# Hybrid encoder trunk on one core: where the score rows live, which engine makes w_out's low parts, and when the pair sums are queued

## The chip, the core and the metric

The kernel runs on one core of a Trainium2 chip. The metric is the device time of one execution in microseconds (us), from runs on the chip; each run gives one time, and the table below gives the median. Beside them stands one profiled execution, whose trace all rows in this document come from.

## What is computed

Two batches, a prompt of 512 tokens and a sample of 1024, go through the same layer of 1024 channels, all in fp32. Cut to what matters:

```
h = rmsnorm(x);  z = h @ w_in                      # q 8 heads x 64, k, v 2 heads x 64, conv 2 x 512
sc = q @ k.T / 8 + bias, |q-k| <= 128              # window: 3 blocks of 128 keys
m = max(max(sc), sink)
p = exp(sc - m);  denom = sum(p) + exp(sink - m)   # one sink logit per head
a = (p / denom) @ v
c = silu(layernorm(dwconv31(ca * sigmoid(cb))))
x = x + concat(a, c) @ w_out
h = rmsnorm(x);  u = dwconv3(h @ w_up)             # 2 x 2816 columns
x = x + (silu(u[:2816]) * u[2816:]) @ w_down
y = rmsnorm(x)
```

## The kernel before

**Products.** Every fp32 operand of a large product is split into a high part (a copy rounded by ScalarE, ACT) and a low part (the difference, made by VectorE, DVE, or GpSimd, POOL). Each 128-deep step of a product is three matmuls, hi·hi, hi·lo and lo·hi. `split` (from L139) does this for a weight: the cast is L142, the subtraction L143, on DVE if `dve` is true and on POOL otherwise. `proj` (L249 to L252) issues the three matmuls for eight steps.

**Stages, with their place in the trace.** Up to about 117 us: projections of the prompt. 117 to some 376: projections of the sample as the main work, with `prompt()` beside it (attention of four blocks of 128 queries in eight units of one block and one key head, conv_norm of the convolution half, the prompt's w_out product). 300 to 680: the prompt's feed-forward up-projection (`ffn_step`) as the main work, with `sample()` beside it (attention of the sample in 16 units, the loads and splits of w_out, two conv_norms). 668 to 793: the sample's w_out product, blocks 4 to 11 of 128 rows (`out_blocks`), with conv_norm, the `pair_sums` and the first transposes beside it. 793 to 816: the turn to a wide form of the sample's up-projection, which takes sums and differences of row blocks and of weight blocks in place of one product (`scaled`, `sums_up`, `turned`, `prod` with its matmuls at L1002 to L1004). Then that up-projection and the down-projections to the end.

**What sets the order.** The main work calls `tick` after every second step of a product. `tick` adds `pace["rate"]` to an account and calls the next part of the generator at the head of `side` for each whole unit on it; the convolution taps have an account of their own. A scheduler then fixes the order in which each engine takes its instructions; on an engine it is a fixed queue, and an instruction that waits holds up all behind it. The same holds for SP's queue, which issues the DMAs. A DMA's start waits until the tile that it writes is free.

**Memory.** SBUF tiles are slots of fixed size, taken by size: 15 of 4096 bytes per partition (names q), 4 of 4224 (c), 61 of 2048 (h), 2 of 2176 (d) and 32 small ones (s). A raw weight and its two parts take a q slot each. Where h slots have run out, an h-sized tile takes a larger one. PSUM banks have the names a, u, b, c.

**Scores.** `scores` (from L496) issues two matmuls a head (L512) and one DVE instruction (L514) that adds the bias, keeps the negated sum in a row of SBUF and gives the row's minimum. In that row, column 0 holds the negated sink logit, put there once by eight DVE copies in `sink_columns` (L490), so that one exp on ACT (L523) over row and sink gives p and its sum with the sink's share. The rows are four tiles of 4096 bytes (`score_rows`, two heads each), held through the prompt's attention and again through the sample's. DVE then takes the reciprocal (L526), and ACT and POOL scale p. In `values`, TensorE turns p (L553), ACT and DVE split it (L555, L556), and TensorE multiplies it with v (L567, L568).

**conv_norm** (from L600) loads rows of the convolution, transposes them (L612), takes mean and variance on DVE, the reciprocal deviation on POOL (`rstd_of`, L126 and L127), normalizes on DVE (L618), transposes back (L624) and applies the activation on ACT (L627 to L631).

**w_out.** `split_wo` splits the sixteen 512-wide pieces of w_out. In `sample()` the argument `m % 4 < DW2` sends half of them to DVE; in `prompt()` `kc % 2 < DW` sends all to DVE, with the DW = 2 that the change leaves.

**The up-projection's evacuation.** ACT takes the middle tap of a PSUM bank (L779), DVE adds the two outer taps from the same bank (L775); then the bank is free for the next projection.

**pair_sums** (from L808), eleven of them: two loads of gated values (L811, L812), four 256-wide POOL operations (L816 to L819), four stores (L821). Their results are read in the wide stage. They wait in `side` at the rate RE = 1.4, with conv_norms put ahead of them.

**End of the out stage.** For each block the residual sum (L653), the square sum on ACT (L659), the rstd on POOL (L126, L127) and the scaling on DVE (L900); DVE also makes the weight sums (`sums_up`, L878) and the low parts of the transposes (L925 are the transposes).

Of the kernel before, what the change touches and what calls it, by code (L numbers as in the profile page):

```python
# [12 lines left out]
AF = mybir.ActivationFunctionType  # L13
ALU = mybir.AluOpType

P = 128
# [6 lines left out]
GRP = NH // NKV  # L23
# [13 lines left out]

RA, RB, RBO, RD, RN, RE = 1.2, 0.8, 2.5, 0.8, 0.95, 1.4  # L40


CA, CB = 0.9, 0.4
# [4 lines left out]
SCB, SCD = "aapa", "aaap"  # L48


WOP, WOA, DW, DW2 = 1, 5, 2, 2
NE = 2
YN = 2
OB = "uc"
# [41 lines left out]
def tile_hybrid_encoder(ctx: ExitStack, tc: tile.TileContext, xs, rel_bias, norm_attn_g, w_in,  # L96
                        attn_sink, conv_dw_w, conv_dw_b, conv_ln_g, conv_ln_b, w_out, norm_ffn_g,
                        w_up, ffn_dw_w, ffn_dw_b, w_down, norm_final_g, onehot, outs):
    nc = tc.nc
# [7 lines left out]
    sb = Slots(big, dict(q=(15, 4096), c=(4, 4224), h=(61, 2048), d=(2, 2176), s=(32, 64)))  # L107
# [3 lines left out]
    def sm(n):  # L111
        return sb.tile([n])
# [373 lines left out]
    def sink_columns():  # L486
        for h in range(0, NH, 2):
            t = sb.tile([2, NT])
            for n in range(2):
                nc.vector.tensor_copy(t[:, n, 0:1], nsink[:, h + n:h + n + 1])  # L490
            score_rows.append(t)

    def row_of(h):
        return score_rows[h // 2][:, h % 2, :]

    def scores(u):  # L496
        i, kv = divmod(u, 2)
        load_q(u)
        if blocks[min(u + 1, 2 * NB - 1) // 2][0] is blocks[i][0]:
            load_q(u + 1)  # L500
        G, b = blocks[i]
        kts = window(i)
        k0, nk = kts[0] * P, len(kts) * P
        off = (kts[0] - b + 1) * P
        q = qt.pop(u)
        negm, den = sm(GRP), sm(GRP)
        pr = []
        for j in range(GRP):
            h = kv * GRP + j
            sc = bank("attn")  # L510
            for L in range(2):
                nc.tensor.matmul(sc[:, :nk], q[:, j, :], kt[G["g"], kv][L][:, k0:k0 + nk],  # L512
                                 start=(L == 0), stop=(L == 1))
            nc.vector.tensor_tensor_reduce(  # L514
                out=row_of(h)[:, 1:1 + nk], in0=sc[:, :nk], in1=bias[h][:, off:off + nk], scale=-1.0,
                scalar=nsink[:, h:h + 1], op0=ALU.add, op1=ALU.min, accum_out=negm[:, j:j + 1])
            del sc
            if j == 1:
                yield 0.0

        for j in range(GRP):
            p = sb.tile([1 + 3 * P])
            nc.scalar.activation(p[:, :1 + nk], row_of(kv * GRP + j)[:, :1 + nk], AF.Exp, scale=-1.0,  # L523
                                 bias=negm[:, j:j + 1], accum_out=den[:, j:j + 1])
            pr.append(p)
        nc.vector.reciprocal(den[:], den[:])  # L526
# [178 lines left out]
    use.update(step="b", turn="a", attn="au", norm="au", out="u")  # L705

    def prompt():
        sink_columns()
        yield from attention(0, 8, {u: conv_norm(u - 4) for u in range(4, 8)})
        kt.clear(), vt.clear(), qt.clear(), bias.clear(), score_rows.clear()  # L710
        pace.update(rate=RBO, late=CLO)
        for n in range(2):
            for kc in range(KC):
                if (kc, n) not in wor:
                    load_wo(kc, n)
            yield 0.0
# [91 lines left out]
    def pair_sums(p):  # L808

        e, o, x, y = (sb.tile([NT]) for _ in range(4))  # L810
        nc.sync.dma_start(e[:], gt[2 * p][:])  # L811
        nc.sync.dma_start(o[:], gt[2 * p + 1][:])  # L812
        yield 0.0
        yield 0.0
        gp = nc.gpsimd.tensor_tensor
        gp(x[:, HR], e[:, HR], o[:, HR], op=ALU.add)  # L816
        gp(x[:, HL], e[:, HL], e[:, HR], op=ALU.subtract)
        gp(e[:, HR], x[:, HR], e[:, HL], op=ALU.subtract)
        gp(y[:, HL], o[:, HL], e[:, HR], op=ALU.subtract)  # L819
        for i, src in ((5, x[:, HR]), (7, x[:, HL]), (6, e[:, HR]), (3, y[:, HL])):  # L820
            nc.sync.dma_start(gb[i, p][:], src)  # L821
        yield 0.0
# [756 lines left out]
```

## Time and profile before

| | us |
|---|---|
| three runs | 1581.71, 1574.94, 1573.73 |
| their median | 1574.94 |
| the profiled execution | 1579.13 |
| its span in the trace | 1577.3 |

Its mean granted TensorE clock is 0.982. A row of the timeline reads: start in us, duration in us, engine, line, operation, the tiles out and in by name, their shapes, how many instructions in a row; and in brackets the idle time of the engine ahead of it with what ended it. A row of the table of stretches reads: from and to, length, then the busy us of PE (matmul), PEld (weight load), DVE, ACT and POOL with their instruction counts, the granted PE clock, the share of the DMA engines' time, GB/s. SPq rows are the DMA issues of SP's queue.

### The profile page before, as it was taken

The numbers are of one execution on the slowest core, as the hardware profiler recorded it, in microseconds if no ns is written. First come the engines' busy times: TensorE is split into PE (matmuls) and PEld (weight loads), VectorE is DVE, ScalarE is ACT, GpSimd is POOL, SyncE is SP. The second block draws the span as 40 slices with busy tenths as digits, with TensorE's granted clock in tenths as the row PEclk, the third lists the DMA queues.
The fourth block names the chain that finished last, engine by engine and source line by source line (L and its number), as shares of the span: only waits on it lengthen the run. The fifth ranks groups of instructions, "written<-read, shape, count | busy, mean of one in ns | idle before, by whom it ended". The sixth has DMA issues, their size and how long they took to land. (4 is left out here: it accounts for less than half of the span.)

```text
span 1577.3 us, 20139 instructions
## 1 busy us (share of the span) xinstructions
PE 1517.2 (96%) x6843; PEld 1234.2 (78%) x6843; DVE 1155.5 (73%) x1604; ACT 794.6 (50%) x1396; POOL 711.6 (45%) x558
## 2 busy tenths in 40 slices
PE   8999999799999999899979999999999999999997
PEld 6787778587888888788867888888888788888885
DVE  7998577747888895745776787778876945668883
ACT  4635545435677786624344444544445533343354
POOL 6641334324667765746533555555555000003345
PEclk9999899899999999999989999999999999999999
DMA  7573235328343435778432333333331582356644
GB/s 227 159 193 94 69 107 160 100 96 252 105 129 127 131 124 160 222 231 273 147 110 67 99 103 100 101 100 100 105 119 57 191 303 77 117 158 221 216 151 160
DMA packets 228780, 227.17 MB, mean 144 GB/s; under 512 B 13268, under 2 KB 168348, under 8 KB 228549
## 3 DMA queue, kind: packets, MB, share of 16 engines
q1 hardware_dynamic: 228677, 225.88, 45.2%
q8 instruction: 54, 0.88, 0.2%
q14 instruction: 49, 0.40, 0.1%
HBM read 164.74 MB, written 62.14 MB: 144 GB/s over the span
## 5 line engine op out<-in xcount | busy, mean ns | idle before, releaser
L143 POOL TENSOR_TENSOR q<-q,q 128x1024 fp32r<-128x1024 f32 x71 | 172.2, 2431 | 115.4 <-ACT q L142 43.0
L878 DVE TENSOR_TENSOR h<-h,h 128x512 fp32r<-128x512 f32 (+2 forms) x202 | 155.9, 805 | 64.4 <-ACT h L882 25.6
L878 POOL TENSOR_TENSOR q<-q,q 128x512 fp32r<-128x512 f32 x82 | 114.2, 1404 | 152.9 <-ACT q L988 147.7
L1334 PE MATMUL w<-h,h 128*128 128x512 f32 x462 | 181.3, 392 | 0.5 <-DVE q L1121 0.5
L1335 PE MATMUL w<-h,h 128*128 128x512 f32 x462 | 181.3, 392 | 0.0
L1336 PE MATMUL w<-h,h 128*128 128x512 f32 x462 | 181.2, 392 | 0.0
L249 PE MATMUL u<-h,q 128*128 128x512 f32 x400 | 162.4, 406 | 6.5 <-DVE h L775 4.5
L250 PE MATMUL u<-h,q 128*128 128x512 f32 x400 | 159.6, 399 | 0.0
L252 PE MATMUL u<-h,q 128*128 128x512 f32 x384 | 152.4, 397 | 1.9 <-POOL q L143 1.8
L1002 PE MATMUL w<-h,q 128*128 128x512 f32 x372 | 147.7, 397 | 3.5 <-ACT h L1083 1.6
L1004 PE MATMUL w<-h,q 128*128 128x512 f32 x372 | 147.1, 395 | 0.6 <-POOL q L878 0.6
L292 DVE SCALAR_TENSOR_TENSOR c<-c,cvw,c 128x512 f32<-128x512 f32 x184 | 137.9, 750 | 2.5
L875 POOL TENSOR_TENSOR q<-q,q 128x1024 f32<-128x1024 f32 x12 | 32.9, 2752 | 236.9 <-DVE q L875 220.2
L1003 PE MATMUL w<-h,q 128*128 128x512 f32 x350 | 137.7, 393 | 0.0
L882 ACT CAST h<-h 128x512 fp32r<-128x512 f32 x120 | 71.8, 619 | 95.4 <-DVE h L878 41.2
L249 PE MATMUL b<-h,q 128*128 128x512 f32 x256 | 103.7, 405 | 1.9 <-DVE d L322 1.6
L142 ACT CAST q<-q 128x1024 fp32r<-128x1024 f32 x72 | 75.3, 1050 | 59.5 <-DMA q<-in_w_in 23.9
L1334 PEld LDWEIGHTS w<-h,h 128*128 128x128 f32 x462 | 86.8, 188 | 20.5 <-ACT h L882 0.9
L250 PE MATMUL b<-h,q 128*128 128x512 f32 x256 | 102.1, 399 | 0.0
L1336 PEld LDWEIGHTS w<-h,h 128*128 128x128 f32 x462 | 86.7, 188 | 19.6
L1335 PEld LDWEIGHTS w<-h,h 128*128 128x128 f32 x462 | 86.8, 188 | 19.5
L252 PE MATMUL b<-h,q 128*128 128x512 f32 x240 | 95.9, 400 | 0.0
(427 smaller groups left out, 3819.5 us busy)
## 6 DMA issues: line engine op xcount, KB each, us to landing
q<-in_w_up SPq DMA_DIRECT2D x88, 512.0 KB
ga<-q SPq DMA_DIRECT2D x64, 256.0 KB
h<-ga SPq DMA_DIRECT2D x57, 256.0 KB
q<-in_w_in SPq DMA_DIRECT2D x28, 512.0 KB
h<-in_w_down SPq DMA_DIRECT2D x52, 256.0 KB
q<-in_x_sample SPq DMA_DIRECT2D x15, 512.0 KB
h<-qsd SPq DMA_DIRECT2D x24, 256.0 KB
x1d<-q SPq DMA_DIRECT2D x11, 512.0 KB
```

The source lines that it names most:

```text
L143: (nc.vector if dve else nc.gpsimd).tensor_tensor(lo[:], raw[:], hi[:].bitcast(F32), op=ALU.subtract)
L249: nc.tensor.matmul(out, whi[:, kc, :], hi[:], start=(kc == 0), stop=False)
L250: nc.tensor.matmul(out, whi[:, kc, :], lo[:], start=False, stop=False)
L252: nc.tensor.matmul(out, wlo[:, kc, :], hi[:], start=False, stop=(kc == KC - 1))
L292: nc.vector.scalar_tensor_tensor(acc[:], src(t), w(t), acc[:], op0=ALU.mult, op1=ALU.add)
L878: (eng or nc.vector).tensor_tensor(out, a, b, op=ALU.subtract)
L1002: nc.tensor.matmul(out, whi[:, s], hi[:], start=(start and c == 0), stop=False, **go)
L1003: nc.tensor.matmul(out, whi[:, s], lo[:], start=False, stop=False, **go)
L1004: nc.tensor.matmul(out, wlo[:, s], hi[:], start=False, stop=(stop and c == 3), **go)
L1334: nc.tensor.matmul(out, sh[:, c], th[:], start=(p == 0), stop=False)
L1335: nc.tensor.matmul(out, sh[:, c], tl[:], start=False, stop=False)
L1336: nc.tensor.matmul(out, sl[:, c], th[:], start=False, stop=(p == NPAIR - 1))
```

## The change

Three things. In the prompt's attention the score rows no longer last: each head's row is a fresh tile, the exp is done in it, in place and without the sink's column, and the sink's share is added with two DVE adds and one 128x4 exp per unit; the sample's attention keeps the old way. `DW2` goes from 2 to 0, so that all low parts of the sample's w_out are made on POOL. The rate of the side work is 2.2 in blocks 4 to 7 of the out stage and from block 8 on 0.9 in place of 1.4, so that the pair sums come ahead of block 8.

```
-RA, RB, RBO, RD, RN, RE = 1.2, 0.8, 2.5, 0.8, 0.95, 1.4
+RA, RB, RBO, RD, RN, RE = 1.2, 0.8, 2.5, 0.8, 0.95, 0.9
...
-WOP, WOA, DW, DW2 = 1, 5, 2, 2
+WOP, WOA, DW, DW2 = 1, 5, 2, 0
...
         negm, den = sm(GRP), sm(GRP)
+        lasting = bool(score_rows)
...
+            if lasting:
+                p = row_of(h)
+            else:
+                p = sb.tile([1 + 3 * P])
+                pr.append(p)
             nc.vector.tensor_tensor_reduce(
-                out=row_of(h)[:, 1:1 + nk], in0=sc[:, :nk], in1=bias[h][:, off:off + nk], scale=-1.0,
+                out=p[:, 1:1 + nk], in0=sc[:, :nk], in1=bias[h][:, off:off + nk], scale=-1.0,
                 scalar=nsink[:, h:h + 1], op0=ALU.add, op1=ALU.min, accum_out=negm[:, j:j + 1])
...
+        if lasting:
...
+        else:
+            es = sm(GRP)
+            nc.vector.tensor_tensor(es[:], sinkb[:, kv * GRP:(kv + 1) * GRP], negm[:], op=ALU.add)
+            for j in range(GRP):
+                nc.scalar.activation(pr[j][:, 1:1 + nk], pr[j][:, 1:1 + nk], AF.Exp, scale=-1.0,
+                                     bias=negm[:, j:j + 1], accum_out=den[:, j:j + 1])
+            nc.scalar.activation(es[:], es[:], AF.Exp)
+            nc.vector.tensor_tensor(den[:], den[:], es[:], op=ALU.add)
         nc.vector.reciprocal(den[:], den[:])
...
     def prompt():
-        sink_columns()
         yield from attention(0, 8, {u: conv_norm(u - 4) for u in range(4, 8)})
-        kt.clear(), vt.clear(), qt.clear(), bias.clear(), score_rows.clear()
+        kt.clear(), vt.clear(), qt.clear(), bias.clear()
...
     side.extend(pair_sums(p) for p in range(NPAIR))
+    pace.update(rate=2.2)
     for i in range(4, NB - 2):
         if i + NE < NB:
             side.appendleft(conv_norm(i + NE))
         if i == 8:
+            pace.update(rate=RE)
             side.appendleft(turned(1, old_bank))
```

The order of the instructions moves on every engine. The new lines push later ones down: from `scores` on, a line of before has 15 or 16 more in the changed kernel, so that L612 is L628, L567 is L583, L775 is L790, L878 is L893.

On TensorE, near the end of the prompt's attention, the kernel before has this (L612 and L624 are conv_norm's transposes, L567 and L568 products with v, L648 to L650 the first w_out matmuls, L249 to L252 projection):

```order
L252 MATMUL b_149_2652<-h_105_649,q_402_2503 128x512
L624 MATMUL u_144_2544<-ident,q_406_2525 128x128 x4
L612 MATMUL a_150_2680<-ident,h_428_2672 128x128 x4
L567 MATMUL a_148_2610<-h_413_2590,h_162_954 128x512
L624 MATMUL u_152_2714<-ident,h_432_2692 128x128 x4
L568 MATMUL a_148_2610<-q_414_2591,h_162_954 128x512
L567 MATMUL a_148_2610<-q_415_2606,h_162_954 128x512
L568 MATMUL a_148_2610<-q_416_2607,h_162_954 128x512
L648 MATMUL u_154_2827<-h_448_2779,h_218_1313 128x512
L649 MATMUL u_154_2827<-h_449_2780,h_218_1313 128x512
```

The changed kernel has at the same place:

```order
L252 MATMUL b_149_2672<-h_105_649,q_406_2523 128x512
L628 MATMUL a_150_2700<-ident,h_432_2692 128x128 x4
L583 MATMUL a_148_2630<-h_417_2610,h_162_954 128x512
L584 MATMUL a_148_2630<-q_418_2611,h_162_954 128x512
L583 MATMUL a_148_2630<-q_419_2626,h_162_954 128x512
L584 MATMUL a_148_2630<-q_420_2627,h_162_954 128x512
L249 MATMUL b_153_2829<-h_83_525,q_427_2668 128x512
L250 MATMUL b_153_2829<-h_84_526,q_427_2668 128x512
L249 MATMUL b_151_2726<-h_125_739,q_405_2522 128x512
```

The conv_norm transposes of u_152, which stood between the products with v, come 30 projection matmuls later, after the first of w_out's matmuls; the projection of b_153 with the weight q_427 has moved ahead.

On DVE, where the sample's w_out is split (L775 are the taps of the up-projection's banks, L577 an attention output), before:

```order
L143 TENSOR_TENSOR h_1053_6509<-h_1026_6415,h_1052_6508 128x512
L775 SCALAR_TENSOR_TENSOR h_1012_6362<-u_358_6315,fw,h_1012_6362 128x511
L143 TENSOR_TENSOR h_1062_6540<-h_1038_6462,h_1061_6539 128x512
L775 SCALAR_TENSOR_TENSOR h_1012_6362<-u_358_6315,fw,h_1012_6362 128x511
L143 TENSOR_TENSOR h_1070_6574<-h_1043_6478,h_1069_6573 128x512
L143 TENSOR_TENSOR h_1040_6465<-h_1023_6402,h_1039_6464 128x512
L143 TENSOR_TENSOR h_1085_6644<-h_1063_6549,h_1084_6643 128x512
L143 TENSOR_TENSOR h_1075_6593<-h_1060_6537,h_1074_6592 128x512
L577 TENSOR_TENSOR h_1011_6349<-b_360_6331,h_989_6218 64x512
L775 SCALAR_TENSOR_TENSOR h_1035_6447<-u_362_6380,fw,h_1035_6447 128x511 x2
```

And in the changed kernel, the same taps and attention output:

```order
L572 TENSOR_TENSOR h_1013_6348<-a_359_6342,h_1012_6347 128x512
L790 SCALAR_TENSOR_TENSOR h_1016_6382<-u_358_6335,fw,h_1016_6382 128x511 x2
L593 TENSOR_TENSOR h_1015_6369<-b_360_6351,h_993_6238 64x512
L790 SCALAR_TENSOR_TENSOR h_1039_6467<-u_362_6400,fw,h_1039_6467 128x511 x2
L816 SCALAR_TENSOR_TENSOR b_364_6542<-b_364_6542,h_1039_6467 128x512
```

The subtractions of L143 are gone from between the taps; they stand on POOL.

On POOL at the end of the out stage, before (L816 to L819 are pair sums, L126 and L127 the rstds of blocks 10 and 11, L878 low parts of the wide stage's weights):

```order
L878 TENSOR_TENSOR h_1276_7734<-q_1_7526,h_1275_7733 128x512
L817 TENSOR_TENSOR h_1248_7550<-h_1246_7548 128x256
L816 TENSOR_TENSOR h_1248_7550<-h_1246_7548,h_1247_7549 128x256
L818 TENSOR_TENSOR h_1246_7548<-h_1248_7550,h_1246_7548 128x256
L819 TENSOR_TENSOR h_1249_7551<-h_1247_7549,h_1246_7548 128x256
L126 TENSOR_SCALAR rs_153<-s_1270_7719 128x1
L127 TENSOR_TENSOR rs_153<-rs_153,nhalf 128x1
L878 TENSOR_TENSOR c_1342_8243<-q_5_8159,c_1342_8243 128x512
L126 TENSOR_SCALAR rs_153<-s_1283_7776 128x1
L127 TENSOR_TENSOR rs_153<-rs_153,nhalf 128x1
```

The same rstds in the changed kernel:

```order
L893 TENSOR_TENSOR h_1278_7745<-q_1_7588,h_1277_7744 128x512
L893 TENSOR_TENSOR h_1284_7757<-q_3_7592,h_1283_7756 128x512
L893 TENSOR_TENSOR h_1282_7753<-q_3_7592,h_1281_7752 128x512
L893 TENSOR_TENSOR c_1346_8263<-q_5_8179,c_1346_8263 128x512
L126 TENSOR_SCALAR rs_153<-s_1270_7721 128x1
L127 TENSOR_TENSOR rs_153<-rs_153,nhalf 128x1
L126 TENSOR_SCALAR rs_153<-s_1287_7796 128x1
L127 TENSOR_TENSOR rs_153<-rs_153,nhalf 128x1
```

No pair sum is left among the last rows; the two rstds stand side by side behind the weights' low parts.

More of the change, by code (lines that the diff above doesn't have):

```diff
@@ L519, in scores @@
                 yield 0.0
[L521 to L525, printed above, removed]
+        if lasting:
+            for j in range(GRP):
+                p = sb.tile([1 + 3 * P])
+                nc.scalar.activation(p[:, :1 + nk], row_of(kv * GRP + j)[:, :1 + nk], AF.Exp, scale=-1.0,
+                                     bias=negm[:, j:j + 1], accum_out=den[:, j:j + 1])
+                pr.append(p)
+        else:
+            es = sm(GRP)
+            nc.vector.tensor_tensor(es[:], sinkb[:, kv * GRP:(kv + 1) * GRP], negm[:], op=ALU.add)
+            for j in range(GRP):
+                nc.scalar.activation(pr[j][:, 1:1 + nk], pr[j][:, 1:1 + nk], AF.Exp, scale=-1.0,
+                                     bias=negm[:, j:j + 1], accum_out=den[:, j:j + 1])
+            nc.scalar.activation(es[:], es[:], AF.Exp)
+            nc.vector.tensor_tensor(den[:], den[:], es[:], op=ALU.add)
         nc.vector.reciprocal(den[:], den[:])
```

## The prediction

> **What bounds the kernel now.** I read first the busy share of each engine on the page, then a table of stretches of the span (length, busy time of PE, PEld, DVE, ACT and POOL, granted PE clock, DMA share, GB/s), then the waits and the timeline of the stretches where TensorE loses time.
>
> ```profile
> PE 1517.2 (96%) x6843; PEld 1234.2 (78%) x6843; DVE 1155.5 (73%) x1604; ACT 794.6 (50%) x1396; POOL 711.6 (45%) x558
> ```
>
> TensorE is the bound of the whole. An edit on another engine can only take away time that TensorE idles or runs at a lower clock.
>
> ```profile
> 150.00:165.00 15.00, 11.66 (x47) 8.73 (x47) 13.06 (x25) 9.18 (x21) 4.86 (x3) 0.77 0.45 114
> 165.00:176.00 11.00, 8.87 (x40) 6.82 (x40) 9.20 (x18) 5.84 (x14) 2.49 (x2) 0.97 0.16 49
> 222.00:232.00 10.00, 6.77 (x30) 4.88 (x29) 9.65 (x18) 6.79 (x16) 2.87 (x2) 0.72 0.62 170
> 272.00:292.00 20.00, 10.53 (x41) 7.04 (x40) 11.95 (x20) 8.95 (x17) 8.30 (x11) 0.73 0.33 95
> 300.00:600.00 300.00, 298.24 (x1407) 246.42 (x1407) 236.28 (x429) 193.26 (x357) 175.63 (x115) 1.00 0.43 134
> 656.00:664.00 8.00, 5.89 (x19) 4.42 (x18) 6.63 (x7) 7.28 (x11) 4.07 (x3) 0.79 0.65 222
> 664.00:674.00 10.00, 7.57 (x27) 5.77 (x26) 8.96 (x9) 1.93 (x4) 7.36 (x4) 0.83 0.46 151
> 790.00:800.00 10.00, 7.84 (x36) 6.17 (x36) 4.24 (x6) 1.69 (x3) 5.28 (x8) 1.00 0.54 185
> 800.00:816.00 16.00, 10.13 (x42) 7.88 (x42) 14.70 (x20) 7.51 (x14) 6.50 (x5) 0.68 0.20 66
> ```
>
> I take the loss of a stretch as its length less PE busy time × granted clock. It is an estimate: a part of the busy time at full clock overlaps. Prompt attention: 15 − 11.66×0.77 = 6.0; 11 − 8.87×0.97 = 2.4; 10 − 6.77×0.72 = 5.1; 20 − 10.53×0.73 = 12.3; together 25.8 us. The w_out splits at the end of the sample's attention: 3.35 + 3.7 = 7.05. The end of the out stage: 2.2 + 9.1 = 11.3. In all 44 us, in the very places that the change touches. Between them the table shows a TensorE that is full (298.24 of 300): nothing is to be had there.
>
> **Part 1: the prompt's scores.** Removed: eight copies of the sink column and four 4 KB slots per partition held through the prompt's attention. Added per unit (eight units): two small DVE adds and one 128x4 exp between the last exp and the reciprocal. What the slots may be worth stands at 272 to 292, in the timeline (start, us, engine, line, waits in brackets):
>
> ```profile
> 275.50 0.39 PE L250 MATMUL b<-h,q 128*128 128x512 f32 x1
> 275.73 0.39 PE L252 MATMUL b<-h,q 128*128 128x512 f32 x1
> 279.02 0.66 PE L624 MATMUL u<-ident,q 128*128 128x128 f32 x4 [2.90 <-DVE q L618]
> 285.85 0.80 PE L567 MATMUL a<-h,h 128*128 128x512 f32 x1 [5.74 <-ACT h L555]
> 285.22 0.57 ACT L555 CAST h<-a 128x512 fp32r<-128x512 f32 x1
> 291.48 1.04 ACT L142 CAST q<-q 128x1024 fp32r<-128x1024 f32 x1
> 292.59 2.38 POOL L143 TENSOR_TENSOR q<-q,q 128x1024 fp32r<-128x1024 f32 x1 [8.57 <-ACT q L142]
> 280.14 1.17 SPq L673 DMA_DIRECT2D h<-in_w_out  x2
> 281.47 0.47 SPq L136 DMA_DIRECT2D q<-in_w_in  x1
> ```
>
> TensorE issues a 512-wide matmul every 0.23 us, and after 275.73 it has no projection to issue: the next weight comes late, since its load stands in SP's queue behind w_out loads (281.47), so its cast is at 291.48 and its low part at 292.59. In between TensorE has only the attention's short chains, and waits out each of them (2.90, 5.74). With four more slots the changed order issues that load earlier, and 30 matmuls of a projection (30×0.23 = 6.9 us) stand between the same value and transpose groups. I take 12.3 down to 1.5: **gain 11**. The three earlier groups (13.5 us) keep clusters of short steps in the new order, so I take nothing there. Bounds for the part: 0 (each cluster that goes comes back elsewhere, as rival 1 has it) to 22 (all but 4 of 25.8).
>
> The added operations have their nearest rows in the reciprocal of the same shape, and in the exps of the same unit (count, then min/median/max ns, below them who made the reciprocal wait):
>
> ```profile
> L526 DVE RECIPROCAL s<-s x8: 160/174/179, 125.7 to 258.9; 128x4 f32<-128x4 f32 x8
>   ACT h L523: 5.4, 2
> L523 ACT ACTIVATION_READ_ACCUMULATOR h<-q,s x28: 185/187/204, 124.0 to 253.1; 128x1 f32 x28
> ```
>
> Two adds at 0.17 and an exp at about 0.19 make 0.53 us a unit, 4.2 in all, 0.35 of each unit behind the last exp (the other add runs beside the exps). TensorE has projections to issue meanwhile, except in the clusters; three of eight units uncovered at 0.5 make **+1.5**, between 0 and 4.2. The price where the cover is gone: the added wait on ACT stands in DVE's in-order queue, ahead of the convolution taps and the PSUM evacuations of the projections; the reciprocal's waits show what one costs, 5.4/2 = 2.7 us each.
>
> **Part 2: the low parts on GpSimd.**
>
> ```profile
> 643.72 0.69 DVE L143 TENSOR_TENSOR h<-h,h 128x512 fp32r<-128x512 f32 x1 [0.59 <-POOL h L805]
> 652.19 4.41 DVE L143 TENSOR_TENSOR h<-h,h 128x512 fp32r<-128x512 f32 x1
> 657.96 0.75 DVE L775 SCALAR_TENSOR_TENSOR h<-u,fw,h 128x511 f32<-128x511 f32 x1 [1.36 <-ACT h L779]
> 659.89 7.99 DVE L143 TENSOR_TENSOR h<-h,h 128x512 fp32r<-128x512 f32 x4
> 652.41 2.38 POOL L143 TENSOR_TENSOR q<-q,q 128x1024 fp32r<-128x1024 f32 x1
> 654.76 1.29 POOL L143 TENSOR_TENSOR h<-h,h 128x512 fp32r<-128x512 f32 x1
> 659.98 2.83 POOL L143 TENSOR_TENSOR q<-q,q 128x1024 fp32r<-128x1024 f32 x1 [3.93 <-ACT q L142]
> ```
>
> The waits of TensorE in that stretch (us in total, times, longest):
>
> ```profile
> PE u L249 <- DVE h L775: 4.5, 2, 2.4
> ```
>
> On DVE the subtraction takes 0.69 alone, but 4.41 and 4 in 7.99 where POOL runs its own subtractions: the first ends at 656.60, beside POOL's pair that ends at 656.05. The taps that empty the banks for TensorE stand behind it, and TensorE waits for them 4.5 us, twice, and loses clock after. The changed DVE queue has none of these eight there. The Trainium skill, "SBUF — State Buffer", section "Who interferes with whom", says that a VectorE instruction with two SBUF inputs blocks fully against a GpSimd one that reads SBUF, and one with a single SBUF input doesn't; the rows agree, and by it the taps, which read PSUM, stay at their 0.75 however much POOL does.
>
> POOL pays 8×1.29 = 10.3 us. It has idle time to give (3.93 before 659.98 alone), but two weights of the up-projection pass through the same queue, at 2.4 each, behind the moved ones; I count a residual of 2.5 of the 7.05, between 0 and 7: **gain 4.5**. The skill speaks against the edit: "GPSIMD Engine Reference", section "4.1 Engine selection", has two-input elementwise work about twice as slow on GpSimd and says to use VectorE. The rows show 1.29 against 0.69; by that rule the sum would lose 8×0.6 = 4.8 here instead, which is my upper residual and rival 2.
>
> **Part 3: the pair sums earlier.** Nothing is added; 44 POOL sums, 22 loads and 44 stores move from the whole out stage to its first four blocks.
>
> ```profile
> 787.98 1.06 ACT L659 ACTIVATE h<-q 128x1024 bf16<-128x1024 f32 x1 [1.50 <-DVE q L653]
> 788.95 0.19 ACT L659 ACTIVATION_READ_ACCUMULATOR h<-q 128x1 f32 x1
> 793.59 0.19 POOL L126 TENSOR_SCALAR rs<-s 128x1 f32<-128x1 f32 x1
> 793.86 0.55 POOL L127 TENSOR_TENSOR rs<-rs,nhalf 128x1 f32<-128x1 f32 x1
> 795.76 1.33 DVE L878 TENSOR_TENSOR h<-q 128x512 f32<-128x512 f32 x1 [7.82 <-DMA gb<-h]
> 797.01 1.40 DVE L900 SCALAR_TENSOR_TENSOR c<-q,rs,q 128x512 f32<-128x512 f32 x2
> 799.07 0.66 PE L925 MATMUL b<-ident,q 128*128 128x128 f32 x4 [2.16 <-DVE h L878]
> 805.14 3.41 DVE L900 SCALAR_TENSOR_TENSOR q<-c,rs,q 128x512 f32<-128x512 f32 x2 [0.72 <-POOL rs L127]
> 809.80 0.69 PE L925 MATMUL t<-ident,q 128*128 128x128 f32 x2 [5.62 <-DVE h L878]
> ```
>
> Block 10's sum of squares is there at 789.14, its rstd is made at 793.59, behind the last pair's sums on POOL; DVE stands 7.82 us at a sum that needs the slot of the last pair, until its stores have landed; everything DVE does for the turn comes late, and TensorE waits 2.16 and 5.62. With the pairs gone by then, DVE starts its chain some 6 us sooner. What is late next is block 11's own chain behind its last matmul: the residual sum, 0.7 like any 512-wide DVE operation here, the square (1.06 + 0.19), the rstd (0.19 + 0.55), half of the two scalings (1.40/2), 3.4 in all, and four hand-overs between engines, an estimate of 0.8: 4.2. In the changed order 15 matmuls of the wide stage, 3.5 us, cover it. So 11.3 falls to about 2.3, the difference of 0.7 and the clock and first weights behind it: **gain 9**, between 5 and 10.
>
> ```profile
> 700.00:740.00 40.00, 39.65 (x190) 32.20 (x189) 19.08 (x26) 11.80 (x25) 23.57 (x37) 1.00 0.94 306
> ```
>
> The moved transfers meet DMA engines that are 94% busy in the middle of the out stage already; TensorE is full there all the same (39.65 of 40), and nothing waits for a pair before the wide stage. I count 0 for that, at worst half the gain, in which conv_norm's loads and rstd stand behind the pairs.
>
> **Sum.** −11 + 1.5 − 4.5 − 9 = −23 us: the profiled execution of 1579.1 becomes 1556. Against the median shown, 1574.94, 4 us lower than that execution, it is **1552**.
>
> **The rivals.** 0.5% of this kernel, about 8 us, is what its measurement can tell from no change.
>
> *1: the prompt's attention gives its gain back.* The 30 matmuls that now cover the cluster at 272 are missing somewhere else, since TensorE's work in the stage is the same. For it: four clusters exist and the change moves one. Against: the last was starved by a load's place in a queue, not by a lack of work. Time: 1552 + 11 = 1563. Chance 0.16.
>
> *2: GpSimd becomes the bound* of the splits and of blocks 4 to 7, by the twofold price: 4.5 gained becomes 0, and conv_norm's rstd behind the pair sums cost half of the 9. Time: 1552 + 4.5 + 4.5 = 1561. Chance 0.12.
>
> *3: both come true*, or the schedule on the chip gives the waits back under other names: 1552 + 11 + 9 to 1552 + 23, about 1573. Chance 0.12.
>
> *4: slower, by the added wait in DVE's queue.* In the prompt's attention DVE is 87 to 97% busy (13.06 of 15, 9.65 of 10) while TensorE stands. If the wait for the exp of es, 2.7 us twice a group and the clock that it costs, makes each of the four groups like the dearest, they lose 4×12.3 = 49.2 in place of 25.8, +23.4, less 13.5 from the other parts: +10, 1585. It decides for slower from 11.8 us a group on (4×11.8 = 47.3, which is 21.5 more, less 13.5: +8). Against: the queue before already waits for the exps at this place. Chance 0.08.
>
> **How the numbers follow.** My forecast has 0.52. It runs from 1575 − 22 − 7 − 10 = 1536 to about 1562; with rivals 1 and 2 (1561, 1563) that is 0.80. The upper end, 1571, takes in the unknown costs of those two (the 4.2 of the added operations, the residual of 7 on POOL). Faster by over 0.5% (under 1567): 0.52 + 0.16 + 0.12 = 0.80. Within: rival 3, 0.12. Slower: rival 4, 0.08.
>
> **What would show it.** Right: no stretch in the prompt's attention like that at 272 (PE under 60% busy, clock 0.73); the weight load there ahead of w_out's; no DVE L143 of several us near 650 and no PE wait for L775 there; block 10's rstd within 1 us of its square, and a PE wait under 2 us at the last transposes. Wrong: new PE waits for DVE reciprocals or exps of es; a weight's low part on POOL late near 665; PE waits on conv_norm's rstd beside blocks 4 to 7; the loss of the prompt's stage still over 20.

## The result, and the profile after

The changed kernel takes 1567.82 us (median of 8 runs, 1566.32 to 1571.12) beside 1576.57 of the kernel before in the same runs (8 runs, 1573.73 to 1581.71). The ratio is 0.9943, interval 0.9928 to 0.9959: some 9 us faster, where 23 were forecast and the range ended at 1571. The sign was right, the size was not. Each part was then run alone, and all ratios below are to the kernel before in the same job:

| kernel | ratio | interval | us of 1576.6 |
|---|---|---|---|
| all three parts | 0.9943 | 0.9928 to 0.9959 | -9.0 |
| part 1 alone (score rows) | 0.9961 | 0.9947 to 0.9976 | -6.1 |
| part 2 alone (low parts on GpSimd) | 1.0053 | 1.0040 to 1.0066 | +8.4 |
| part 3 alone (pair sums earlier) | 0.9948 | 0.9934 to 0.9963 | -8.2 |
| parts 1 and 3 | 0.9897 | 0.9882 to 0.9911 | -16.2 |

Part 3 does what was forecast of it, near enough, and part 1 brings 6 of its 9.5. Part 2 was forecast at -4.5 and costs 7 to 8: that by difference (0.9943 less 0.9897), this alone. Most of the missing time is there.

Where it shows in the trace of the changed kernel: first the same table of stretches as before the change, for the places that lose time now (columns as there).

```profile
150.00:176.00 26.00, 23.59 (x119) 18.96 (x116) 24.01 (x49) 17.28 (x41) 8.28 (x6) 1.00 0.42 122
215.00:235.00 20.00, 18.36 (x94) 14.84 (x93) 10.17 (x23) 14.38 (x31) 7.56 (x6) 1.00 0.58 140
243.00:261.00 18.00, 14.21 (x48) 10.15 (x48) 15.94 (x31) 10.59 (x24) 0.93 (x1) 0.72 0.53 147
262.00:300.00 38.00, 37.21 (x172) 29.83 (x171) 16.72 (x24) 19.07 (x33) 21.19 (x16) 1.00 0.52 146
361.00:372.00 11.00, 5.60 (x20) 4.12 (x19) 4.04 (x7) 7.48 (x11) 5.43 (x4) 0.70 1.00 335
655.00:667.00 12.00, 7.93 (x23) 5.74 (x22) 4.16 (x6) 2.84 (x5) 11.94 (x8) 0.72 0.55 169
685.00:692.00 7.00, 4.81 (x26) 3.86 (x24) 2.95 (x5) 4.04 (x9) 2.63 (x4) 1.00 1.09 371
715.00:735.00 20.00, 16.47 (x69) 12.52 (x68) 9.52 (x12) 4.83 (x10) 14.24 (x19) 0.91 0.88 291
786.00:806.00 20.00, 18.11 (x91) 13.99 (x89) 16.24 (x24) 9.16 (x17) 6.06 (x9) 1.00 0.30 103
```

Length less PE busy time × clock, as in the prediction: the prompt's attention loses 2.4, 1.6, 7.8 and 0.8 in its four rows. The group at 272 is gone, the one at 243 is new to the list, and the earlier ones, which lost 13.5 before, lose 4.0. 361 to 372 loses 7.1: that is the start of the up-projection. The split loses 12 - 7.93×0.72 = 6.3, hardly less than the 7.05 of before. 685 to 692 and 715 to 735 lose 2.2 and 5.0; these are the out stage's first blocks, where the kernel before was full:

```profile
684.00:712.00 28.00, 28.00 (x132) 22.93 (x131) 10.59 (x16) 6.09 (x13) 11.44 (x16) 1.00 0.75 243
712.00:735.00 23.00, 22.65 (x107) 18.11 (x106) 13.22 (x17) 7.89 (x16) 15.29 (x24) 1.00 0.91 297
```

And the turn (786 to 806) loses 1.9, where it lost 11.3.

A second way to see it, which serves for the runs below. Every trace here has 6843 matmul records, so the start of the record with a given number can be compared between two traces; the difference at the borders of the stages gives what each stage gained (-) or lost (+) against the profiled execution of before, in us. The first stage carries some noise: kernels whose prompt stage is the old one (part 2 alone, part 3 alone) show -4.4 and -1.7 in it. So a difference of 2 or 3 us between two traces in one stage is to be read with care.

| trace | to 1500: prompt's attention and w_out | to 1600: start of the up-projection | to 2900 | to 3000: split of w_out | to 3400: out stage | to 3600: turn |
|---|---|---|---|---|---|---|
| all three parts | -14.3 | +6.0 | -0.2 | -0.5 | +7.3 | -9.0 |
| part 1 alone | -14.5 | +5.1 | -0.2 | +0.6 | +2.3 | +0.7 |
| part 2 alone | -4.4 | -0.1 | +0.2 | -1.6 | +10.2 | 0.0 |
| part 3 alone | -1.7 | +0.4 | 0.0 | +0.2 | +4.0 | -11.5 |
| parts 1 and 3 | -16.3 | +4.9 | -0.1 | +0.2 | +4.2 | -11.5 |

The main waits of TensorE in the changed kernel (waiting operation, who was waited for, us, times, longest); the first at 350 to 380 us, the second at the split, the next two in the out stage, the last at the turn.

```profile
PE u L249 <- ACT h L210: 5.4, 1, 5.4
PE u L249 <- DVE h L790: 4.1, 2, 3.2
PE u L664 <- DVE s L631: 2.2, 1, 2.2
PE a L628 <- DMA h<-cvd: 1.7, 1, 1.7
PE t L940 <- DVE q L915: 1.3, 1, 1.3
```

L790 is the L775 of before: the waits for the taps that emptied the banks, 4.5 us in two, are 4.1 in two, although no subtraction of L143 stands on DVE between them any more.

### The profile page after: what moved, and what is told of

Read it like the earlier page. It is cut to its first block, busy times and chain, and to the rows that moved or that the text cites. A ratio compares the mean times of both kernels' runs of the same rounds, so it can differ in the third digit from the quotient of the medians.

```text
span 1565.5 us, 20161 instructions
## 1 busy us (share of the span) xinstructions
PE 1512.7 (97%) x6843; PEld 1231.3 (79%) x6843; DVE 1139.0 (73%) x1604; ACT 795.7 (51%) x1404; POOL 717.8 (46%) x566
## 5 line engine op out<-in xcount | busy, mean ns | idle before, releaser
L143 POOL TENSOR_TENSOR q<-q,q 128x1024 fp32r<-128x1024 f32 x72 | 173.6, 2419 | 85.9 <-ACT q L142 29.0
L893 DVE TENSOR_TENSOR h<-h,h 128x512 fp32r<-128x512 f32 (+2 forms) x202 | 157.5, 812 | 67.3 <-ACT h L897 25.6
L893 POOL TENSOR_TENSOR q<-q,q 128x512 fp32r<-128x512 f32 x82 | 116.6, 1434 | 156.2 <-ACT q L1003 150.8
L249 PE MATMUL u<-h,q 128*128 128x512 f32 x400 | 162.5, 407 | 10.7 <-ACT h L210 5.4
L252 PE MATMUL u<-h,q 128*128 128x512 f32 x384 | 152.4, 397 | 1.7 <-POOL q L143 1.7
L249 PE MATMUL b<-h,q 128*128 128x512 f32 x256 | 103.2, 403 | 3.5 <-DVE d L322 1.8
L250 PE MATMUL b<-h,q 128*128 128x512 f32 x256 | 102.0, 398 | 0.0
L252 PE MATMUL b<-h,q 128*128 128x512 f32 x256 | 101.9, 399 | 0.0
```

What stands on the lines that cost most here:

```text
L143: (nc.vector if dve else nc.gpsimd).tensor_tensor(lo[:], raw[:], hi[:].bitcast(F32), op=ALU.subtract)
L249: nc.tensor.matmul(out, whi[:, kc, :], hi[:], start=(kc == 0), stop=False)
L250: nc.tensor.matmul(out, whi[:, kc, :], lo[:], start=False, stop=False)
L252: nc.tensor.matmul(out, wlo[:, kc, :], hi[:], start=False, stop=(kc == KC - 1))
L893: (eng or nc.vector).tensor_tensor(out, a, b, op=ALU.subtract)
```

## The experiments

### Each part alone, and two of the three

Part 1 alone is the diff without its two `pace.update` lines, with RE = 1.4 and `DW2 = 2`. Part 2 alone is one number, part 3 alone the rates:

```
part 2:  -WOP, WOA, DW, DW2 = 1, 5, 2, 2      part 3:  -... RN, RE = ... 0.95, 1.4
         +WOP, WOA, DW, DW2 = 1, 5, 2, 0               +... RN, RE = ... 0.95, 0.9
                                                       +    pace.update(rate=2.2)      # ahead of block 4
                                                       +            pace.update(rate=RE)   # at block 8
```

> Part 1 alone: the prompt's score rows no longer last, all else as in the kernel before. Theory A (the parts add up as their places in the changed trace show): the prompt's stage gains 14.2 us and the start of the up-projection gives 6 back, so 1576.6 - 8.3 = 1568.3, with one TensorE wait of over 5 us at the first up-projection matmul and no other new one. Theory B (the wait at the up-projection comes from the other two parts, through the one schedule): 1576.6 - 14.2 = 1562.4, without that wait.

> Part 2 alone: the sample's w_out low parts all on GpSimd. Theory A: the old waits behind DVE's subtractions go and waits behind ACT's w_out casts come, so 0.5 us less, 1576, within noise of before; out stage as before. Theory B (the loss beside blocks 4 to 7 in the changed kernel comes from GpSimd being late with the splits, not from the pair sums): 1576.6 - 0.5 + 7 = 1583, with waits of TensorE between the split and block 8. The forecast's own step (waits gone, 4.5 gained): 1572.

> Part 3 alone: side work at 2.2 in blocks 4 to 7, then 0.9. Theory A: 9 us gained at the turn, 7.3 lost in the first blocks to conv_norms whose loads and deviations stand behind pair sums, so 1576.6 - 1.7 = 1575. Theory B: the pair sums cost nothing there, 1576.6 - 9 = 1567.6.

> Parts 1 and 3 without part 2. Theory A: 1576.6 - 8.3 - 1.7 = 1566.6, some 1 us from the changed kernel (1567.8). Theory B: 1576.6 - 14.2 - 9 = 1553, since the two new losses came from part 2.

Measured: 1570.97, 1585.15, 1568.53 and 1560.90 us, with the ratios of the table above. Part 1 gains in its stage and gives 5 back at the up-projection's start all by itself, as theory A had it; that is why parts 1 and 3 come out between the two forecasts (1566.6 and 1553). But part 2 alone is slower than the kernel before, clear of noise, and parts 1 and 3 without it are 7 us faster than with it: theory B, that the loss in the out stage comes from GpSimd's low parts, holds for a part of it. Part 2 alone loses 10.2 there, but part 3 alone loses 4.0 and parts 1 and 3 lose 4.2, without part 2. Read finer, the changed kernel loses 6.4 from record 3040 to 3240 (blocks 4 to 6) and 1.3 from there to 3400 (blocks 7 to 9), parts 1 and 3 lose 0.3 and 3.9. So part 2 adds its loss in blocks 4 to 6; in blocks 7 to 9 it loses less than they do, and at the turn it gains 2.5 less. The waits of TensorE from 640 to 790 us, first part 2 alone, then parts 1 and 3:

```profile
PE a L624 <- DVE h L618: 4.4, 3, 2.8
PE u L249 <- DVE h L775: 4.0, 2, 3.2
PE u L648 <- DVE s L615: 2.2, 1, 2.2
```

```profile
PE u L249 <- DVE h L790: 6.5, 2, 4.0
PE a L628 <- DMA h<-cvd: 1.7, 1, 1.7
```

In part 2 alone the new waits stand in conv_norm (L618 and L634 normalize, L624 and L640 turn back) and in the first out block (L648), some 20 to 70 us behind the last of the subtractions that were moved.

### How many subtractions, how early, and the wait at the up-projection's start

Four edits, three of them to find which property of part 2 costs, one on the wait that part 1 hands on:

```
half:         DW2 = 1, parts 1 and 3            all on DVE:   DW2 = 4, parts 1 and 3
early start:  RN = 1.25, all three parts        K/V late, parts 1 and 3:
-    load_kv()
     drain(convs)
...
+        if k == 1:
+            load_kv()
         if k == U0:
             side.append(sample())
```

> Parts 1 and 3, with DW2 = 1: four of the eight subtractions go to GpSimd and four stay on DVE. Theory P (the loss of part 2 is GpSimd's work: its queue is fuller and conv_norm's deviations come late): half of the 6.9, 1560.9 + 3.5 = 1564.4. Theory S (the loss is the order: with the low parts on GpSimd the scheduler puts the first conv_norms and out blocks behind the last projections, where TensorE has nothing to cover their chains): the order here has the out blocks right behind the conv_norm transposes as the changed kernel has, so about the whole loss, 1567.

> Parts 1 and 3, with DW2 = 4: all sixteen subtractions on DVE. Theory P: GpSimd is freer still, no loss in the out stage, and DVE's blocked subtractions cost twice what they cost before (7 us more): 1560.9 + 7 = 1568 with the loss at the split. Theory S: the out stage is that of parts 1 and 3 since its order is nearly the same; GpSimd has only the up-projection's weights to subtract, so DVE is blocked less per subtraction, and the split costs about what it did: 1561.

> The changed kernel with RN = 1.25 in place of 0.95, so that w_out's loads and splits and the first conv_norms start earlier beside the prompt's up-projection; as many subtractions on GpSimd as in the changed kernel. Its order has 24 projection matmuls between the first conv_norm's second transposes and the second conv_norm's first. Theory S: the loss of part 2 goes, 1567.8 - 7 = 1561. Theory P: GpSimd has the same work, 1567 to 1568.

> Parts 1 and 3 (1560.9), and the loads of the sample's keys and values moved from the first step of the up-projection to its second. In the trace of parts 1 and 3 the first up-projection matmul waits 4.9 us for ACT, which waits for the up-projection's weight, 11 to 13 us from issue to landing among 3 MB of keys and values. Theory T (the traffic makes the weight late): the wait and the half clock after it go, 1560.9 - 5 = 1556. Theory Q (the weight is late because its load is issued late, behind the stores of the w_out blocks in SP's queue): no change, 1561.

Measured: half 1560.52 (0.9902, 0.9884 to 0.9920), all on DVE 1564.96 (0.9926, 0.9911 to 0.9941), early start 1584.75 (1.0049, 1.0035 to 1.0064), K/V late 1573.11 (0.9964, 0.9948 to 0.9981).

Theories P (the amount of work on GpSimd) and S (the first conv_norms without projections to cover them) both miss their times: half costs nothing where they had 1564 and 1567, and the early start, which has the cover back, is 17 us slower than the changed kernel, where S had 1561. All on DVE comes out between the two (1568 and 1561). The waits of TensorE tell more. Half, 640 to 790 us:

```profile
PE a L628 <- DMA h<-cvd: 4.1, 2, 2.2
PE a L640 <- DVE h L634: 1.9, 1, 1.9
PE u L249 <- DVE h L790: 1.0, 1, 1.0
```

The early start has seven rows of waits over 1.5 us in the same stretch, for the taps (6.2 in three), for DVE's scaling, for ACT, for conv_norm's rows.

With four of the eight moved, the split gains 5.8 us (records 2900 to 3000), a little more than the forecast's 4.5; one wait of 1.0 is left of the two. The out stage then loses 7.2, 3.0 more than parts 1 and 3 lose there, so that half costs nothing in sum only because the split pays for it: the work on GpSimd has a price behind the split here too. The largest wait there is for conv_norm's rows from memory (L628 waits for the load from `cvd`). That pointed to the loads.

K/V late takes the wait at the up-projection's start away (+0.3 in place of +4.9), but it moves two things at once. By the DMA semaphores of the traces, the weight that the first cast waits for is issued at 350.4 us in parts 1 and 3 and lands 9.4 us later; with the keys and values out of the way it is issued at 345.6 and lands 5.3 us later. Of the 8.9 us that it comes sooner, 4.1 are the lighter traffic (theory T) and 4.8 the earlier place in SP's queue, which theory T did not have; the run does not tell which of the two would have been enough. And the keys and values come late in turn (the second row). Waits of TensorE at 350 to 400 us:

```profile
PE u L249 <- DVE h L789: 3.8, 1, 3.8
PE a L513 <- DMA q<-ksd: 2.3, 1, 2.3
```

Records 1600 to 2900 lose 7.8, and the kernel is slower by 12 than without the edit. The trace shows 8 of them; the twelve runs spread from 1563.8 to 1576.4, and the profiled one, 1566.5, is among the fastest, so the rest is not accounted for.

### Who holds conv_norm up

Two theories were left: deviations behind pair sums in GpSimd's queue (P2), or loads behind the pair sums' stores in SP's queue (Q). Two edits, each on all three parts and on parts 1 and 3:

```
-        gp = nc.gpsimd.tensor_tensor                   # P2: sums on DVE
+        gp = nc.vector.tensor_tensor

-            nc.sync.dma_start(gb[i, p][:], src)        # Q: stores issued by ACT
+            nc.scalar.dma_start(gb[i, p][:], src)
```

> The changed kernel (1567.8) with the pair sums' four additions on DVE in place of GpSimd, which leaves GpSimd in the out stage with little but the deviations. Theory P2 (part 2's loss beside blocks 4 to 7 is made of deviations that stand behind pair sums in GpSimd's queue, with DVE's scalings and conv_norms behind them): most of the loss goes, 1567.8 - 5 = 1563. Theory Q (conv_norm's loads stand in SP's queue behind pair-sum stores that wait for the sums): the sums come as late on DVE, 1567 to 1569.

> Parts 1 and 3 (1560.9) with the pair sums on DVE: the same edit without part 2. Theory P2: little to be had here, 1559 to 1561, so the distance to the run with part 2 and the same edit falls from 6.9 to about 2. Theory Q: no change, distance still 7.

> The changed kernel (1567.8) with the pair sums' 44 stores issued by ACT in place of SP, so that no load of conv_norm stands behind a store that waits for a pair sum; the order of the out stage on TensorE is nearly that of the changed kernel. Theory Q: the waits for conv_norm's rows go and the loss shrinks by about 5, 1563. Theory P2: the deviations come as late as before, 1567 to 1569, and later if ACT has to wait for GpSimd.

> Parts 1 and 3 (1560.9) with the pair sums' stores issued by ACT. Theory Q: the 1.7 us wait for conv_norm's rows at 750 us and the waits beside it go, 1560.9 - 3 = 1558. Theory P2: no change, 1561.

| | all three parts | parts 1 and 3 | what part 2 costs |
|---|---|---|---|
| unedited | 0.9943 (0.9928 to 0.9959) | 0.9897 (0.9882 to 0.9911) | 0.0046, 7 us |
| sums on DVE | 0.9951 (0.9937 to 0.9964) | 0.9922 (0.9910 to 0.9935) | 0.0029, 5 us |
| stores on ACT | 0.9914 (0.9899 to 0.9928) | 0.9900 (0.9887 to 0.9914) | 0.0014, 2 us |

In us the four were 1568.49, 1564.85, 1563.23 and 1561.60. The last column is a difference of two ratios and is uncertain by about 0.002, 3 us.

The sums on DVE do not settle P2. It said 1563 and gets 1568.5, but the edit has a price of its own, 4 us on parts 1 and 3, and TensorE's wait at the first out block grows from 2.2 to 4.4 us. The distance, 5 us, lies between P2's 2 and Q's 7.

The stores on ACT speak for Q, with two reservations. Q said 1563 for all three parts and gets 1563.2, and part 2 then costs 2 us in place of 7; but for parts 1 and 3 it said 1558 and gets 1561.6, although the wait of 1.7 for conv_norm's rows is gone there too. And by the traces the gain stands in blocks 4 to 6 (records 3040 to 3240 lose 1.6 in place of 6.4), while 3.2 of it come back in blocks 7 to 9 (4.5 in place of 1.3). Of the 5.9 us by which the last matmul comes sooner in the trace, 3.3 lie ahead of record 2900, where TensorE's order is the same: that is noise. So the loss beside blocks 4 to 6 is made of something that the edit takes away; that 5 us of part 2's cost go with it is the middle value of a wide interval. SP's waits in the changed kernel at 685 to 735 us, of L836, the pair sums' stores, for GpSimd:

```profile
SPq L836 <- POOL h L831: 5.8, 7, 2.6
SPq L836 <- POOL h L832: 3.5, 7, 1.0
SPq L836 <- POOL h L833: 2.5, 4, 1.3
```

11.8 us in three rows, in which nothing behind them in the queue is issued; the same three are 3.2, 0.8 and 1.5, 5.5 in all, in the trace of parts 1 and 3. There the stores wait for other things instead: all rows of L836 together are 15.2 us in the changed kernel and 13.0 in parts 1 and 3. The length of the stand alone doesn't tell the two apart. The timeline of the changed kernel around one of the waits (start, us, engine, line, waits in brackets): block 4's rstd on GpSimd among pair sums, DVE's scaling L911 that waits for it with conv_norm's L634 behind, the load of conv_norm's rows issued at 716.75 among the stores, and TensorE.

```profile
712.89 0.19 POOL L126 TENSOR_SCALAR rs<-s 128x1 f32<-128x1 f32 x1
714.83 0.55 POOL L127 TENSOR_TENSOR rs<-rs,nhalf 128x1 f32<-128x1 f32 x1
715.42 1.28 DVE L911 SCALAR_TENSOR_TENSOR q<-q,rs,q 128x1024 f32<-128x1024 f32 x1 [4.61 <-POOL rs L127]
716.75 0.53 SPq L622 DMA_DIRECT2D h<-cvd  x1
719.88 0.68 PE L628 MATMUL a<-ident,h 128*128 128x128 f32 x4 [1.69 <-DMA h<-cvd]
720.79 0.63 PE L664 MATMUL u<-h,h 128*128 128x512 f32 x1
721.21 0.63 PE L665 MATMUL u<-h,h 128*128 128x512 f32 x1
```

That load stood in the queue behind stores, but the last stretch of its delay is its own. The issue ahead of it ended at 715.22, and it then waited at the head of the queue, by the profile for 1.3 us until pair-sum stores had landed (waits of SP, the longest last):

```profile
SPq L622 <- DMA gb<-h: 1.4, 2, 1.3
```

A pair sum's tiles are h slots, as the load's tile is, and they are free only when the stores that read them have landed. So there is a second way from the pair sums to conv_norm's rows, through the slots, which neither Q nor P2 named; the stores on ACT can shorten both, and no run here separates them.

With the stores issued by ACT, the same stretch is nearly full, and the wait for the rows is gone from the list of waits at 680 to 790 us, whose longest is the 2.2 of L664:

```profile
715.00:735.00 20.00, 19.20 (x87) 15.05 (x86) 7.95 (x11) 8.00 (x17) 14.59 (x21) 1.00 0.92 308
```

The 2.2 that stays (TensorE at 688 us in the changed kernel, a first out block that waits for a bank whose taps are still being read) stands with the same length in part 2 alone and in both of these with the stores on ACT, and in no trace with four or none of the subtractions moved. In that order the last projection and the run of out matmuls have only eight transposes between them. That it comes from the order is read, not tried; the early start, with another order, doesn't have it.

### The same edit on part 2 alone, on the kernel before, and on half

> Part 2 alone (1.0053 of the kernel before, 1585) with the pair sums' stores issued by ACT. Theory Q (part 2's loss in the out stage is made of loads that stand in SP's queue behind stores that wait for pair sums): the loss there, 9.9 us by the trace, shrinks as in the changed kernel by about 5: 1580, 1.002 of before. If Q holds only together with the early pair sums of part 3: 1585, as without the edit.

> The kernel before with the pair sums' stores issued by ACT, the control. Theory Q: the out stage of before has one wait of 0.35 us up to the turn, so nothing is to be had there; at the turn DVE still waits for the last pair's stores: 1576 to 1577, ratio 1.00. If stores on ACT are a gain by themselves, whatever the low parts: 1572, as in the changed kernel.

> Parts 1 and 3 with DW2 = 1 (1560.5, four subtractions on GpSimd) and the pair sums' stores issued by ACT. By the trace of DW2 = 1 the split gains 6 us and the out stage gives 5.7 back, 4.1 of it in two waits for conv_norm's rows. Theory Q: those two go, 1560.5 - 4 = 1556.5. Otherwise 1560 to 1561.

Measured: part 2 alone 1583.42 (1.0038, 1.0020 to 1.0055), the kernel before 1581.71 (1.0038, 1.0019 to 1.0056), half 1557.99 (0.9879, 0.9850 to 0.9909). By the difference to its control part 2 costs nothing once the stores are off SP's queue, where it cost 0.0053 with them on it, which is the direction of Q. But the control itself became slower, which no theory had, and the times of this job spread by 12 to 13 us, so these two don't settle more than the direction; the out stage of part 2 alone loses 5.6 by its trace in place of 10.2, that of the control 3.8.

Half with the stores on ACT has the lowest time of the study; beside half without the edit the middle values show a gain of 2.5 us (3.6 by the ratios, 0.9902 and 0.9879), where Q forecast 4, and the intervals overlap. Only one of the two waits that Q had going went:

```profile
PE a L628 <- DMA h<-cvd: 2.8, 1, 2.8
```

This is the one at 685 us, 2.2 long without the edit. It is there with no pair-sum store in SP's queue, so not every late load of conv_norm's rows is of Q's kind.

## Why the prediction was wrong, point by point

**What bounds the kernel** was right: all time that moved, moved in the places where TensorE waits or runs at a lower clock.

**Part 1, -11 and +1.5.** Right in size for the stage and wrong for what comes behind it. The stage gains 14.5 against the profiled execution of before, some 3 of it noise by the kernels that keep the old stage. That this meets the 11 is in part luck. The group at 272 went, as forecast, and the weight's load is issued ahead of w_out's (275.37 and 275.86). But a group that loses 7.8 came up at 243, as rival 1 would have it, and the three earlier groups, from which I took nothing, lose 9.5 less. Nor was the load's place in SP's queue the whole reason at 272: by the semaphores of the trace, both loads of that weight group (issued at 267.7 and 281.5) had landed by 285.4, and the cast at 291.48 stood in ACT's queue behind casts of w_out.

The 0.19 that I took for the exp is the row of the exps' accumulator read, not of an exp; the added exp measures 0.205, so nothing came of it. It cost nothing to speak of: L541, the add behind it, waited 0.23 us in the group at 243.

The step that failed was one that I didn't make: what is late next when the stage ends 14 us sooner. It is the up-projection's first weight:

```profile
351.51 0.54 SPq L136 DMA_DIRECT2D q<-in_w_up  x1
362.29 1.05 ACT L142 CAST q<-q 128x1024 fp32r<-128x1024 f32 x1 [7.53 <-DMA q<-in_w_up]
367.25 1.83 ACT L210 ACTIVATE h<-a,vecs 128x512 fp32r<-128x512 f32 x3
367.98 1.22 PE L249 MATMUL u<-h,q 128*128 128x512 f32 x2 [5.40 <-ACT h L210]
```

Its load takes 10.8 us from issue to landing among the keys and values, and ACT stands at its cast with the transposes' evacuations (L210) behind it. 5 us go back there; by the K/V run the traffic and the load's place in SP's queue have about equal parts in it. Net, part 1 brought 6 where 9.5 were in the sum.

**Part 2, -4.5.** The failed step of the sum: that TensorE's waits for the taps go when the subtractions leave DVE's queue, and that GpSimd's added work has no price behind the split. The part that I could see in the trace was right: no subtraction of several us is left on DVE, the taps keep their 0.75. But the waits did not go. The prediction has the tap "behind" the subtraction in DVE's queue; its own row of the tap at 657.96 says that DVE waited 1.36 us there for ACT (L779), the subtraction being done at 656.60. In the kernel before, ACT's middle tap stood behind a cast of w_out which in turn waited for DVE's subtraction:

```profile
656.63 0.62 ACT L142 CAST h<-h 128x512 fp32r<-128x512 f32 x1 [3.54 <-DVE h L143]
657.16 0.77 ACT L779 ACTIVATE h<-u,vecs,fw 128x512 f32<-128x512 f32 x1
```

With eight moved, TensorE waits 4.1 us for the same taps, and ACT's middle tap (L794) is late behind the same kind of cast, which now waits for its piece of w_out from memory:

```profile
656.27 0.62 ACT L142 CAST h<-h 128x512 fp32r<-128x512 f32 x1 [1.54 <-DMA h<-in_w_out]
657.84 0.77 ACT L794 ACTIVATE h<-u,vecs,fw 128x512 f32<-128x512 f32 x1
658.64 1.53 DVE L790 SCALAR_TENSOR_TENSOR h<-u,fw,h 128x511 f32<-128x511 f32 x2 [0.52 <-ACT h L794]
660.32 0.76 PE L249 MATMUL u<-h,q 128*128 128x512 f32 x1 [3.17 <-DVE h L790]
```

With four moved the forecast gain is there (5.8 at the split). And I counted GpSimd's extra 10.3 us only where they are spent. Their price is paid later, above all in blocks 4 to 6 (6.4 lost where parts 1 and 3 lose 0.3): 7 us in sum by the runs. By the middle values 5 of them go with the pair sums' stores, which hold up conv_norm's loads; the interval of that is wide. Of the 14 us that the change fell short of its forecast (23 against 9) part 2 makes 11.7, from -4.5 to +7.2; part 1 alone fell 3.4 short of its 9.5. Rival 2 named GpSimd and blocks 4 to 7, with a chance of 0.12, but had at most the gain of part 2 lost and half of part 3's, and nothing below nought for part 2.

The rule of the Trainium skill that I set beside it, "GPSIMD Engine Reference", section "4.1 Engine selection", gave the right sign. The loss of 4.8 that I worked out by it went into neither place that I named for it: the upper residual is 7, and rival 2 has the gain at 0. And the slower engine does not explain the order of the runs: 12 of the 16 subtractions on GpSimd cost no more than 8 (1560.5 beside 1560.9), and none on it is slower than 8 (1565.0 beside 1560.9).

**Part 3, -9.** Right in sum: 8.2 alone. In the trace it is 11.5 at the turn and 4.0 given back in blocks 7 to 9, where I had taken 0 and named half of the gain as the worst case; that the two errors, 2.5 too little and 4.0 too much, nearly cancel is luck. Block 10's rstd follows its square within 0.3 us, and block 11's chain leaves a wait of 1.33 where I had 0.7:

```profile
792.15 0.19 ACT L675 ACTIVATION_READ_ACCUMULATOR h<-q 128x1 f32 x1
792.42 0.19 POOL L126 TENSOR_SCALAR rs<-s 128x1 f32<-128x1 f32 x1 [1.06 <-ACT h L675]
793.28 1.41 DVE L915 SCALAR_TENSOR_TENSOR c<-q,rs,q 128x512 f32<-128x512 f32 x2 [2.13 <-POOL rs L127]
800.28 0.33 PE L940 MATMUL t<-ident,q 128*128 128x128 f32 x1 [1.33 <-DVE q L915]
```

**Rivals 1, 3 and 4.** Rival 1 came true in part: a group came back within the stage (7.8 at 243), though its sum held, and 5 came back in another stage than it had it. Rival 3 (all given back) and rival 4 (the added exp makes each group dear) did not happen; 4×11.8 there is 47.2, not 47.3, which changes nothing.

**What stays open**: what in part 2 makes blocks 4 to 6 lose time. It is not a backlog of subtractions, since the last of them ends well ahead of the out stage's lossy stretches, and GpSimd then has nothing to do for 8.1 and for 7.7 us, the second time until a pair's load has landed (in the changed kernel's timeline):

```profile
670.03 1.29 POOL L143 TENSOR_TENSOR h<-h,h 128x512 fp32r<-128x512 f32 x1 [0.52 <-ACT h L142]
679.45 1.29 POOL L820 TENSOR_TENSOR h<-h,h 128x512 f32<-128x512 f32 x1 [8.13 <-DVE s L631]
689.37 0.72 POOL L831 TENSOR_TENSOR h<-h,h 128x256 f32<-128x256 f32 x1 [7.70 <-DMA h<-gt]
```

That leaves the order in which the sums, their loads and stores, conv_norm's loads and the deviations stand, which the change moves on every queue, and the slots that they hand on; no run held that order fixed, so this is argued and not shown. Open too are why the early start is so slow (its out stage loses 25.9 by the trace), and whether the last 2 us of part 2 are the order's.

## What to carry to other kernels

A step that is moved to another engine joins a queue, and the queue's other work is what pays: here the subtractions cost little where they run, and 7 us later on, a part of it because loads for TensorE came behind, or waited for, the stores of that engine's other work. So follow not only the engine that takes the work, but the stores that wait for it, the loads that stand behind them in the queue of DMA issues, and the slots that they free. Before a wait is put down to one instruction, read what the row of the late one waited for: here ACT's queue stood ahead of DVE's, and relieving DVE left ACT late. Where a stage is made shorter, look up the next weight's load and ask whether it comes sooner too. And change such things one by one: of three edits that went in together, one cost almost half of what the other two brought, and leaving it out (1560.9), or moving half as much with the stores on another queue (1558.0), beats both kernels.

## What the runs showed of the hardware beside this

A wait's length alone did not tell whether the clock goes down. In the changed kernel the single wait of 2.19 us at 688 was followed by matmuls at the full rate, while the waits of 0.36 and 1.69 us at 717 to 720 were followed by matmuls 0.42 us apart (720.79 to 721.21 above), not 0.23, until 723.8, eight of them, which cost 8×0.2 = 1.6 us, as much again as the longer wait itself. It is one pair of places in one trace. The first of the two:

```profile
690.53 0.47 PE L664 MATMUL u<-h,h 128*128 128x512 f32 x1 [2.19 <-DVE s L631]
690.84 0.39 PE L665 MATMUL u<-h,h 128*128 128x512 f32 x1
691.07 0.40 PE L666 MATMUL u<-h,h 128*128 128x512 f32 x1
```
